# Tying the cached-sequence work of a decoder step to the attention blocks beside which it is emitted

## The chip, the cores and the metric

The kernel runs on one core of a Trainium2 chip. The metric is the device time of one execution in microseconds; the number for a kernel is the median of its runs. TensorE multiplies matrices, VectorE (DVE), ScalarE (ACT) and GpSimd (POOL) do the elementwise work, and most transfers are issued by SyncE (SP).

## The reference

One step of a small decoder: a recurrent layer (RG-LRU) and an attention layer (FoX) with a decay between positions. It is done for one new sequence of 2048 tokens (the prompt) and for 8 running sequences of 8 new tokens each, which have 4096 earlier tokens in a paged cache. 16 heads of 64. Cut to what matters here:

```python
def fox_block(q, k, v, cq, ck, q_pos, k_pos):
    s = jnp.einsum('bqhd,bkhd->bhqk', q, k).astype(jnp.float32) * (HEAD_DIM ** -0.5)
    s = s + jnp.swapaxes(cq, 1, 2)[:, :, :, None] - jnp.swapaxes(ck, 1, 2)[:, :, None, :]
    mask = k_pos[None, :] <= q_pos[:, None]
    s = jnp.where(mask[None, None], s, -jnp.inf)
    p = jax.nn.softmax(s, axis=-1)
    return jnp.einsum('bhqk,bkhd->bqhd', p.astype(v.dtype), v)

def run_group(x, rnn_state, conv_state, past_k, past_v, past_logf, pos0, ...):
    ...                     # recurrent layer, then shared keys and values of the new tokens
    k_all = jnp.concatenate([past_k.astype(k_new.dtype), k_new], axis=1)
    v_all = jnp.concatenate([past_v.astype(v_new.dtype), v_new], axis=1)
    ...
    y = fox_mixer(rms_norm(x, b_pre_norm[l]), k_all, v_all, cq, ck, q_pos, k_pos, b_w_in[l], b_w_out[l])
    x = x + rms_norm(y, b_post_norm[l])
```

`run_group` is called twice: for the prompt without a past, and for the running sequences with `cache_k[page_table]` and `cache_v[page_table]` as the past.

## The kernel before, in words

The kernel is written with a planner: the program emits instructions with tiles, and the planner then fixes the order of each engine's queue. It keeps a model of time; an engine takes the instruction emitted earliest among those whose data are ready in that model. Instructions emitted late can therefore be placed early. `together` emits a run of matmuls that stays together behind its first one. At run time each queue is in order.

The stages, in order: the recurrent layer of the first half of the tokens; the shared projections (`shared`, keys, values, queries, gate) of that half; the recurrent layer of the second half; its projections, in two parts of 512 tokens; the attention of the prompt (`attention`); the output projection (`project`).

The attention goes over 64 units, one for each head and each quarter `qc` of the queries. A unit has up to 16 score blocks of 128 keys by 512 queries: two matmuls into `st` (lines 1531 and 1532, and 1534 on the diagonal), the exponential on ScalarE into `p` (1540), and, for four blocks at a time and two blocks later, the products with the values into `ops` (1551) and the sums on GpSimd into `acc`. There are 640 score blocks. Ahead of a unit, `top` makes its row maxima: a matmul into `sx` (1404) and a reduction on VectorE, 1406 off the diagonal and 1408 on it. `top` runs up to 18 blocks ahead (`LEAD`). Score blocks rotate over two PSUM banks, `sx` over three, and `p` over 5 buffers (`NP`). Two more banks, tags `d` and `o`, belong to the decode and later to the projection.

The decode is the attention of the 8 running sequences to the cache. It has 16 turns, one for each sequence and half of the heads; two run beside the projections of the first half, 14 beside those of the second half and the attention. A turn loads 8 groups of 4 key pages and 8 of 4 value pages (`pages`, line 1072; a group is 1 MB, and keys and values share four `raw` buffers). Each key group is transposed by two instructions on VectorE (1157); after four groups, `scores` multiplies (1125 into `dS`). `softmax` follows, with a trip through DRAM (`pd`, `sx`), and then each value group is multiplied by `products` (1235 into `dO`), which waits for the four page transfers themselves. The turns overlap: `period` interleaves the keys of the next turn with the values of this one.

`Side` decides beside what the decode is emitted. `along` adds up the cost that the main work yields, and advances the decode until its own yielded cost is that sum times a share. The decode's cost units are `QK`, `PV` and `HOP`; a turn counts as `TURN` units:

```python
    QK, PV, HOP = 700.0, 255.0, 300.0
    TURN = 16 * QK + 33 * PV + 10 * HOP
```

The share is one number for the projections of the second half and for the attention; what isn't emitted by the end of the attention is emitted after it. After the decode, the same side work loads and splits the output projection's weights (`project_ready`).

Of the kernel before, what the change touches and what calls it, by code (L numbers as in the profile page):

```python
# [11 lines left out]
F32 = mybir.dt.float32  # L12
# [4 lines left out]
AX = mybir.AxisListType  # L17
# [3 lines left out]
P = 128  # L21
# [6 lines left out]
H = 16  # L28
# [15 lines left out]
B_ORDER += [("g", c) for c in range(4)]  # L44

SHARE = 1.13
LEAD = 18
RAMP = 8
NS = 3
# [2 lines left out]
AHEAD = 8  # L52
FIRST = 2
NACC = 5
NP = 5
ADD = "G"
OG = 1
NQ = 6
# [14 lines left out]


SYNC = mybir.DependencyInfo(mybir.DependencyClass.Sync, mybir.DependencyReason.DATA)


def f(ap):
# [5 lines left out]
def tile_hawk_fox(  # L84
# [8 lines left out]
    V, A, G, T, S = nc.vector, nc.scalar, nc.gpsimd, nc.tensor, nc.sync  # L93
# [9 lines left out]
    def tt(eng, out, a, b, op):  # L103
        eng.tensor_tensor(out, a, b, op=op)  # L104

    def together(mms, after=()):

        first = mms[0]().ins
        for d in after:
            tc.add_manual_dep(first, d.ins.name, SYNC)  # L110
        with tc.high_priority(), tc.issue_after(first):
            for mm in mms[1:]:
                mm()
# [97 lines left out]
    psum = {}  # L211
# [805 lines left out]
    TURN = 16 * QK + 33 * PV + 10 * HOP  # L1017
# [4 lines left out]
    def decode(es, turns, nraw, nktr, ahead):  # L1022
# [84 lines left out]
        def keys(t, xs):  # L1107

            dl = t.dl
            b, hg, gmx = t.b, t.hg, t.gmx  # L1110

            def fetch_c():
                sc = t.sc = pool.tile([P, NPG // 4, 8, 32], F32, name="sc", tag="sc")
                S.dma_start(sc[:, :, :, :].rearrange("p x h i -> p (x h i)"),
                            c_d[hg, :, :, b].rearrange("m a x f -> (m a) (x f)").unsqueeze(1).to_broadcast([16, DS, 8 * 256]))
                t.cn = pool.tile([DS, 8, DS], F32, name="cn", tag="cn")
                S.dma_start(t.cn[:, :, :], cn_d[hg * 8:(hg + 1) * 8, b * DS:(b + 1) * DS].unsqueeze(0).to_broadcast([DS, 8, DS]))

            def scores(g, pp, kt):

                sp = bank("dS", "d" if ahead or pp == 0 else "o")

                def score(h, x, a):
                    blk = (h * 2 + x) * 32
                    return T.matmul(sp[a * 32:(a + 1) * 32, h * P:(h + 1) * P], qw[:, pp * 2 + h // 2, h % 2 * 2 + x, :],  # L1125
                                    kt[:, :, a, blk:blk + 32], start=(x == 0), stop=(x == 1))

                together([partial(score, h, x, a) for h in range(4) for x in range(2) for a in range(4)])
                sv = t.sc[:, g * 4:(g + 1) * 4, pp * 4:(pp + 1) * 4, :].rearrange("p n h i -> p h n i")
                tt(V, sv, sp[:, :].rearrange("p (h n i) -> p h n i", h=4, n=4), sv, ALU.subtract)  # L1130
                V.tensor_reduce(gmx[:, g, pp * 4:(pp + 1) * 4], sv, axis=AX.XY, op=ALU.max)

            def new_scores(raw):
                kx = (spare() if ahead else pool.tile([P, 512], F32, name="kx", tag="kx"))[:, :512]
                V.transpose(kx, raw[:, :])
                sp = bank("dS")

                def score(h, x):
                    blk = (h * 2 + x) * 32
                    return T.matmul(sp[:32, h * DS:(h + 1) * DS], qw[:, h // 2, h % 2 * 2 + x, :], kx[:, blk:blk + DS],  # L1140
                                    start=(x == 0), stop=(x == 1))

                together([partial(score, h, x) for h in range(8) for x in range(2)])
                tt(V, t.cn[:, :, :], sp[:DS, :64].rearrange("p (h j) -> p h j", h=8), t.cn[:, :, :], ALU.subtract)
                tt(V, t.cn[:, :, :], t.cn[:, :, :], maskN[:, :].unsqueeze(1).to_broadcast([DS, 8, DS]), ALU.add)
                V.tensor_reduce(gmx[:DS, 2, :], t.cn[:, :, :], axis=AX.X, op=ALU.max)

            for x in xs:
                g, n = divmod(x, 4)
                if n == 0:  # L1150
                    t.kts = [pool.tile([P, 4, 4, 256], F32, name="ktr", tag="ktr", bufs=nktr) for _ in range(2)]
                raw, _ = pages(cache_k, b, hg, x)
                if x == (3 if ahead else 0):
                    fetch_c()
                    t.rown = new_rows(ks_d, b, hg)
                for pp in range(2):
                    V.transpose(t.kts[pp][:, n], raw[:, :, pp * 256:(pp + 1) * 256])  # L1157
                    if n == 3:
                        dl.after(1 + pp, lambda g=g, pp=pp, kt=t.kts[pp]: scores(g, pp, kt))
                    if (g, n, pp) == (1, 0, 0):  # L1160
                        new_scores(t.rown)
                    dl.tick()
                    yield QK
# [59 lines left out]
        def values(t, xs):  # L1223

            dl = t.dl
# [5 lines left out]
            def products(i, raw, came):  # L1231

                def mm(d, a):
                    c = ((i + d) % 2 * 2 + a) * 32
                    return T.matmul(op[c:c + 32, :256], sx[:, d, i // 4, a * 4:(a + 1) * 4, :].rearrange("p h q -> p (h q)"),  # L1235
                                    raw[:, d, a * 256:(a + 1) * 256],
                                    start=(i + d < 2), stop=(i + d == NPG - 1))

                together([partial(mm, d, a) for d in range(4) for a in range(2)], came)

            def new_products(raw):
                for a in range(2):
# [2 lines left out]

            for x in xs:
                raw, came = t.raws.pop(0) if t.raws else pages(cache_v, b, hg, x)
                dl.after(1, lambda i=x * 4, raw=raw, came=came: products(i, raw, came))
                if x == 5:
                    t.rown = new_rows(vs_d, b, hg)  # L1250
                yield 2 * PV
                dl.tick()
                yield 2 * PV
# [53 lines left out]
    def attention(es):  # L1307
# [86 lines left out]
        def top(u, j, ck):  # L1394
# [8 lines left out]
            ps = ps3.tile([P, 512], F32, name="sx", tag="sx", bufs=3)  # L1403
            T.matmul(ps[:, :w], qb[0:96, j * P:(j + 1) * P], kb[0:96, ck * 512:ck * 512 + w], start=True, stop=True)  # L1404
            if ck < qc:
                V.reduce_max(mx[:, j, ck:ck + 1], ps[:, :w], axis=AX.X)  # L1406
            else:
                V.tensor_tensor_reduce(ps[:, :w], ps[:, :w], maskb[:, 512 - w:], scale=1.0, scalar=NEG,
                                       op0=ALU.add, op1=ALU.max, accum_out=mx[:, j, ck:ck + 1])
# [110 lines left out]
            yield 300  # L1520
        ops = acc = None
        pair = []
        for u, (h, qc) in enumerate(units):
            load_low(u + 2)
            for k in range(nks[u]):
# [1 line left out]
                qa, qb = qas[u], qbs[u % NQ]  # L1527
                lo = max(0, k - qc * 4) * P
                ks = slice(k * P, (k + 1) * P)
                ps = ps3.tile([P, 512], F32, name="st", tag="st", bufs=2)  # L1530
                T.matmul(ps[:, lo:], ka[:, ks], qa[:, lo:], start=True, stop=False)  # L1531
                T.matmul(ps[:, lo:], kb[:, ks], qb[:, lo:], start=False, stop=(k < qc * 4))  # L1532
                if k >= qc * 4:
                    T.matmul(ps[:, lo:lo + P], identB[:, :], causal[:, :], start=False, stop=True)
# [41 lines left out]
    lent = {}  # L1576
# [207 lines left out]
    def beside():  # L1784
        yield from decode(dec, turns[FIRST:], 4, 2, True)
        dec.close()
        yield from project_ready(last)

    side = Side(beside())
# [3 lines left out]
    wkeep.close()  # L1793
    lin.close()
    psum["att"] = banks(att, "psa", 6)
    side.along(attention(att), share)
    side.upto(1e12)
    project(last)
    att.close()
# [36 lines left out]
```

## Time and profile before

| what | value |
|---|---|
| median of 3 runs | 3058.37 us (3051.74 to 3059.14) |
| the profiled execution | 3055.27 us, its span 3053.6 us |
| mean granted TensorE clock | 0.965 |
| bytes moved | 653.41 MB, mean 214 GB/s |
| second projections beside decode | about 1210 to 1692 us |
| attention, first to last score block | about 1725 to 2860 us |
| output projection, end | to 3053.6 us |

In the rows of the profile, a group has its line, engine, operation, output and inputs with shapes and count, then after the first bar its busy time and the mean of one in ns, and after the second bar the idle time of the engine just ahead of it and what ended that. The slice rows give tenths of busy time for 40 equal slices of 76.3 us. PE is TensorE's matmuls, PEld its weight loads. Matmul ends are modelled, so a busy PE isn't one at its peak.

### The profile page before, as it was taken

The page shows a single profiled execution, that of the slowest core. Times are in us where ns is not written, and L with a number is a line of the kernel's source. Part 1 is how long each engine was busy: PE and PEld are TensorE (multiplying, and loading weights), DVE is VectorE, ACT ScalarE, POOL GpSimd, SP SyncE. Part 2 cuts the span into 40 slices and gives each one's busy share as a digit, 9 for nine tenths or more (in the row PEclk, how much of TensorE's full clock was granted, in tenths as well). Part 3 has the DMA queues.
Part 4 walks back from the last instruction along what each step waited for, and adds up shares of the span by engine and source line. Part 5 has one row for each costly group of instructions (what it writes and reads, how often), then busy time and mean ns, then how long its engine had stood idle before and what let it go on. Part 6 is the DMA issues. An engine that isn't in the chain of part 4 may idle for free.

```text
span 3053.6 us, 60463 instructions
## 1 busy us (share of the span) xinstructions
PE 2827.0 (93%) x21614; PEld 2258.5 (74%) x21614; DVE 1810.2 (59%) x4012; ACT 1269.8 (42%) x2874; POOL 1079.6 (35%) x1199
## 2 busy tenths in 40 slices
PE   6998999999999989998999799899899899999898
PEld 5997789988999978896888456565556565565687
DVE  7876465425357766765555566676767675554344
ACT  4665442222346655433333144343444345455311
POOL 1653201000016532000000366556465557587522
PEclk9999999999999999999999799899999999999999
DMA  4224546788622256999999988999999998323243
GB/s 122 81 85 133 175 125 203 240 268 263 216 83 89 83 185 194 316 320 320 330 311 315 294 274 268 299 275 308 306 298 319 322 297 258 92 65 86 84 145 111
DMA packets 492864, 653.41 MB, mean 214 GB/s; under 512 B 91099, under 2 KB 292828, under 8 KB 485285
## 3 DMA queue, kind: packets, MB, share of 16 engines
q1 hardware_dynamic: 488934, 643.87, 67.1%
q10 hardware_dynamic: 3340, 3.56, 0.5%
q8 instruction: 171, 2.80, 0.4%
q0 software_dynamic: 288, 2.10, 0.2%
q14 instruction: 131, 1.07, 0.1%
HBM read 513.82 MB, written 135.16 MB: 213 GB/s over the span
## 4 chain that ended last, share of the span: by engine, by line
PE 59%; DMA 18%; DVE 9%; ACT 5%; SPq 4%; issue 3%; POOL 2%; DVEq 0%; ACTq 0%; POOLq 0%
PE ops L1551 6%; PE y L368 4%; PE y L366 4%; PE y L367 4%; DMA raw<-in_cache_v_dram 4%; PE kv L366 4%; PE kv L367 4%; PE kv L368 4%; DMA raw<-in_cache_k_dram 4%; PE st L1531 3%; PE sx L1404 3%; PE dO L1235 3%; PE dS L1125 2%; PE st L1532 2%; PE qg L366 2%
## 5 line engine op out<-in xcount | busy, mean ns | idle before, releaser
L104 POOL TENSOR_TENSOR acc<-acc,p 128x512 f32<-128x512 f32 (+3 forms) x576 | 638.7, 1109 | 419.2 <-PE ops L1551 271.1
L1540 ACT ACTIVATE p<-st 128x512 f32<-128x512 f32 (+3 forms) x576 | 289.5, 524 | 404.9 <-PE st L1532 198.8
L1157 DVE STREAM_TRANSPOSE ktr<-raw 128x1024 f32<-128x1024 f32 x256 | 305.7, 1225 | 160.2 <-DMA raw<-in_cache_k_dram 157.8
L1406 DVE TENSOR_REDUCE mxs<-sx 128x1 f32<-128x512 f32 x384 | 253.1, 679 | 119.7 <-PE sx L1404 118.3
L367 PE MATMUL kv<-wl,xh 128*128 128x256 f32 (+3 forms) x1088 | 309.3, 287 | 11.2 <-DVE wl L411 11.0
L366 PE MATMUL kv<-wh,xh 128*128 128x256 f32 (+3 forms) x1088 | 310.8, 290 | 5.9 <-ACT wh L410 5.4
L368 PE MATMUL kv<-wh,xl 128*128 128x256 f32 (+3 forms) x1088 | 309.4, 287 | 0.0
L1531 PE MATMUL st<-qa,ka 128*128 128x512 f32 (+3 forms) x640 | 273.9, 428 | 12.2 <-ACT p L1540 11.0
L1551 PE MATMUL ops<-p,vvt 128*64 128x256 f32 (+1 forms) x2176 | 261.0, 366 | 3.4 <-ACT p L1540 2.8
L1404 PE MATMUL sx<-kbt,qbt 96*128 96x512 f32 (+3 forms) x640 | 236.9, 425 | 26.1 <-DMA qbt<-qd 12.0
L1532 PE MATMUL st<-qbt,kbt 128*128 128x512 f32 (+3 forms) x640 | 239.3, 374 | 0.0
L410 ACT ACTIVATE wh<-wst,gv 128x256 fp32r<-128x256 f32 (+1 forms) x384 | 164.5, 499 | 179.9 <-DMA wst<-in_b_w_in_dram 62.1
L411 DVE SCALAR_TENSOR_TENSOR wl<-wst,gv,wh 128x256 fp32r<-128x256 f32 (+1 forms) x384 | 170.5, 493 | 105.5 <-ACT wh L410 104.0
L1551 PEld LDWEIGHTS ops<-p,vvt 128*64 128x64 f32 x2176 | 161.2, 140 | 92.6 <-issue 22.7
L366 PE MATMUL qg<-xh,wh 128*128 128x384 f32 (+2 forms) x640 | 228.9, 359 | 0.0
L368 PE MATMUL qg<-xh,wl 128*128 128x384 f32 (+2 forms) x640 | 227.4, 356 | 0.0
L367 PE MATMUL qg<-xl,wh 128*128 128x512 f32 (+2 forms) x640 | 226.9, 356 | 0.0
L367 PEld LDWEIGHTS kv<-wl,xh 128*128 128x128 f32 (+1 forms) x1088 | 204.3, 189 | 14.9 <-DVE wl L411 12.6
L366 PEld LDWEIGHTS kv<-wh,xh 128*128 128x128 f32 (+1 forms) x1088 | 204.2, 189 | 12.0 <-ACT wh L410 6.4
L1090 POOL TENSOR_TENSOR qw<-qb,amask 128x128 f32<-128x128 f32 x64 | 29.3, 464 | 509.9 <-PE dS L1125 266.4
L368 PEld LDWEIGHTS kv<-wh,xl 128*128 128x128 f32 (+1 forms) x1088 | 205.6, 189 | 4.1 <-issue 4.1
L1531 PEld LDWEIGHTS st<-qa,ka 128*128 128x128 f32 x640 | 124.0, 194 | 109.9 <-issue 53.0
(297 smaller groups left out, 6370.0 us busy)
## 6 DMA issues: line engine op xcount, KB each, us to landing
raw<-in_cache_k_dram SPq DMA_DIRECT2D x512, 256.0 KB
raw<-in_cache_v_dram SPq DMA_DIRECT2D x512, 256.0 KB
wst<-in_w_kv_dram SPq DMA_DIRECT2D x48, 512.0 KB
wst<-in_b_w_in_dram SPq DMA_DIRECT2D x48, 512.0 KB
xt<-in_x_prompt_dram SPq DMA_DIRECT2D x32, 512.0 KB
wst<-in_a_w_in_dram SPq DMA_DIRECT2D x64, 256.0 KB
out_dram<-kf SPq DMA_DIRECT2D x128, 128.0 KB
sc<-cd SPq DMA_DIRECT2D x16, 1024.0 KB
```

The source lines that it names most:

```text
L104: eng.tensor_tensor(out, a, b, op=op)
L366: T.matmul(ps, lh(k), rh(k), start=(k == 0), stop=False)
L367: T.matmul(ps, lh(k), rl(k), start=False, stop=False)
L368: T.matmul(ps, ll(k), rh(k), start=False, stop=(k == nk - 1))
L411: V.scalar_tensor_tensor(wl[:, k, :], st[:, k, :], gk, f(wh[:, k, :]), op0=ALU.mult, op1=ALU.subtract)
L1157: V.transpose(t.kts[pp][:, n], raw[:, :, pp * 256:(pp + 1) * 256])
L1404: T.matmul(ps[:, :w], qb[0:96, j * P:(j + 1) * P], kb[0:96, ck * 512:ck * 512 + w], start=True, stop=True)
L1406: V.reduce_max(mx[:, j, ck:ck + 1], ps[:, :w], axis=AX.X)
L1531: T.matmul(ps[:, lo:], ka[:, ks], qa[:, lo:], start=True, stop=False)
L1532: T.matmul(ps[:, lo:], kb[:, ks], qb[:, lo:], start=False, stop=(k < qc * 4))
L1540: pair.append((k, lo, p, A.activation(p[:, lo:], ps[:, lo:], AF.Exp)))
L1551: return T.matmul(ops[r * HD:(r + 1) * HD, a0 * P:], vvs[h % 2][:, k, :], p[:, :].rearrange("p (a r c) -> p a r c", a=2, r=2)[:, a0:, r, : ...
```

## The change

The first matmul of each score block of the attention, and each reduction of line 1406, is remembered as the current place on its engine. A decode transpose gets an order edge to the place on VectorE, and the first matmul of a score run and of a product run one to the place on TensorE, so that the planner can't put them ahead of it. An order edge holds within one engine's queue and adds no semaphore. Page loads, the softmax and the runs for the new rows get no edge. Nothing is tied before the attention, and nothing after it.

The share in the attention is worked out anew: what is left of the 14 turns, over 0.9 of the attention's own cost. The `p` buffers go from 5 to 6. The product run of value group 0 of a turn is emitted one tick later in these turns. Once the decode has been emitted, score blocks use the decode's two banks in turn with their own two.

```diff
+SPAN = 0.9
-NP = 5
+NP = 6
+ORDER = mybir.DependencyInfo(mybir.DependencyClass.NoSync, mybir.DependencyReason.DATA)
...
+    place = {}
+
+    def behind(engine, ins):
+
+        if engine in place:
+            tc.add_manual_dep(ins, place[engine].name, ORDER)
+
+    def together(mms, after=(), beside=False):
         first = mms[0]().ins
         for d in after:
             tc.add_manual_dep(first, d.ins.name, SYNC)
+        if beside:
+            behind("T", first)
...
-                together([partial(score, h, x, a) for h in range(4) for x in range(2) for a in range(4)])
+                together([partial(score, h, x, a) for h in range(4) for x in range(2) for a in range(4)], beside=True)
...
-                    V.transpose(t.kts[pp][:, n], raw[:, :, pp * 256:(pp + 1) * 256])
+                    behind("V", V.transpose(t.kts[pp][:, n], raw[:, :, pp * 256:(pp + 1) * 256]).ins)
...
-                together([partial(mm, d, a) for d in range(4) for a in range(2)], came)
+                together([partial(mm, d, a) for d in range(4) for a in range(2)], came, True)
...
-                dl.after(1, lambda i=x * 4, raw=raw, came=came: products(i, raw, came))
+                dl.after(2 if ahead and x == 0 else 1, lambda i=x * 4, raw=raw, came=came: products(i, raw, came))
...
-                V.reduce_max(mx[:, j, ck:ck + 1], ps[:, :w], axis=AX.X)
+                place["V"] = V.reduce_max(mx[:, j, ck:ck + 1], ps[:, :w], axis=AX.X).ins
...
+        wide = [0]
+
+        def scores_bank():
+
+            if dec_done:
+                wide[0] += 1
+                if wide[0] % 2:
+                    return psum["dec"].tile([P, 512], F32, name="st", tag="do"[wide[0] // 2 % 2], bufs=1)
+            return ps3.tile([P, 512], F32, name="st", tag="st", bufs=2)
...
-                ps = ps3.tile([P, 512], F32, name="st", tag="st", bufs=2)
-                T.matmul(ps[:, lo:], ka[:, ks], qa[:, lo:], start=True, stop=False)
+                ps = scores_bank()
+                place["T"] = T.matmul(ps[:, lo:], ka[:, ks], qa[:, lo:], start=True, stop=False).ins
...
     def beside():
         yield from decode(dec, turns[FIRST:], 4, 2, True)
         dec.close()
+        dec_done.append(True)
         yield from project_ready(last)
...
-    side.along(attention(att), share)
+    cost = sum(4.1 * 0.42 * (512 - max(0, k - qc * 4) * P) + 213 for qc in range(4) for k in range(4 * qc + 4)) * H
+    side.along(attention(att), ((16 - FIRST) * TURN - side.spent) / (cost * SPAN))
+    place.clear()
     side.upto(1e12)
```

More of the change, by code (lines that the diff above doesn't have):

```diff
@@ L104, in tt @@
         eng.tensor_tensor(out, a, b, op=op)
-    def together(mms, after=()):
+    place = {}
[3 more added lines that the diff above has]
+    def together(mms, after=(), beside=False):
         first = mms[0]().ins
@@ L1574, in attention @@
                 yield 4.1 * (512 - lo) * 0.42 + (done[0] - before) * 213
-    lent = {}
+    lent, dec_done = {}, []
     rows = [(NSAMP, None, x1s_d[:, :], ys_flat)]
```

## The prediction

> **What bounds the kernel now.** I read the page first (busy shares, slices, chain), then the stretches of the attention, then the groups of instructions and the waits inside them, and last the timeline around single waits. From the page:
>
> ```profile
> PE 2827.0 (93%) x21614; PEld 2258.5 (74%) x21614; DVE 1810.2 (59%) x4012; ACT 1269.8 (42%) x2874; POOL 1079.6 (35%) x1199
> PE   6998999999999989998999799899899899999898
> PEclk9999999999999999999999799899999999999999
> DMA  4224546788622256999999988999999998323243
> PE 59%; DMA 18%; DVE 9%; ACT 5%; SPq 4%; issue 3%; POOL 2%; DVEq 0%; ACTq 0%; POOLq 0%
> ```
>
> TensorE is busy nearly everywhere, but the dips of PE and PEclk lie in slices 19 to 33, where the DMA row is at 9. Then DMA falls to 3 while PE stays at 9. That is the boundary I need: cached-sequence work ("decode") runs beside the attention only up to about 2570 us, and the attention is alone after that. The stretches (columns: stretch, its length, busy time and count of PE, PEld, DVE, ACT, POOL, then clock, DMA share, GB/s), then score blocks (line 1531 alone) and page transposes (line 1157 alone):
>
> ```profile
> 1692.00:1750.00 58.00, 40.41 (x376) 26.58 (x376) 32.91 (x73) 11.11 (x30) 19.28 (x27) 0.71 1.05 310
> 1750.00:2500.00 750.00, 688.21 (x6748) 437.29 (x6748) 510.21 (x1038) 313.25 (x799) 417.00 (x406) 0.95 0.95 297
> 2650.00:2850.00 200.00, 190.14 (x1094) 115.72 (x1092) 85.44 (x205) 105.59 (x234) 159.53 (x145) 0.99 0.30 79
> ```
>
> ```profile
> 1750.00:2500.00 750.00, 166.33 (x386) 75.24 (x387) 0.95 0.95 297
> 2650.00:2850.00 200.00, 63.46 (x149) 28.20 (x149) 0.99 0.30 79
> 1725.00:2500.00 775.00, 173.09 (x401) 78.68 (x402) 0.95 0.95 298
> ```
>
> ```profile
> 1260.00:1692.00 432.00, 82.11 (x69) 0.96 0.98 323
> 1692.00:2500.00 808.00, 180.69 (x151) 0.93 0.96 298
> ```
>
> Alone, a score block with all that belongs to it costs 200 / 149 = 1.342 us. Beside the decode, 386 blocks at that price would be 518 us of the 750. The decode's own TensorE work there is the sum of the groups that write dO, dS, dres, dsum and dm:
>
> ```profile
> L1404 PE MATMUL sx<-kbt,qbt 96*128 96x512 f32 (+3 forms) x386 | 144.4, 423 | 11.0 <-DVE mxs L1406 7.2 <-ACT qbt L1423 2.4 <-DVE mxs L1408 0.3
> L1235 PE MATMUL dO<-raw,sx 128*32 128x256 f32 x1152 | 80.3, 398 | 25.3 <-DMA raw<-in_cache_v_dram 18.2 <-DMA raw<-in_cache_k_dram 3.3 <-DMA sx<-pd 2.2
> L1125 PE MATMUL dS<-ktr,qw 128*32 128x128 f32 x2240 | 69.5, 277 | 4.4 <-DVE ktr L1157 4.4
> L1140 PE MATMUL dS<-sy,qw 128*32 128x8 f32 x288 | 11.3, 179 | 4.3 <-DVE sc L104 4.3
> L1263 PE MATMUL dres<-sel,ob 128*128 128x16 f32 x72 | 9.5, 265 | 0.0
> L1243 PE MATMUL dO<-rawn,dpc 128*32 128x256 f32 x36 | 7.6, 427 | 0.0
> L1203 PE MATMUL dsum<-ddg,ones 128*128 128x64 f32 x18 | 3.5, 277 | 1.5 <-DVE ddg L104 1.5
> L1181 PE MATMUL dm<-ident,dmr 128*128 128x8 f32 x18 | 2.9, 235 | 1.0 <-DVE dmr L1180 1.0
> L1177 PE MATMUL dm<-ident,dmx 128*128 128x128 f32 x9 | 2.5, 276 | 2.1 <-DVE dmx L1175 2.1
> ```
>
> 80.3 + 69.5 + 11.3 + 9.5 + 7.6 + 3.5 + 2.9 + 2.5 = 187 us for 1152 / 128 = 9 turns, 20.8 us a turn. What is left, **750 - 518 - 187 = 45 us, is the excess of running the two together**, and it is all that this change can win in that stretch. It has two parts. Idle: 750 - 688.2 = 61.8, of which attention alone would have had 386 x (200 - 190.1) / 149 = 25.5, so 36 are extra; the rows above name them (25.3 ahead of the value products, nearly all on pages that had not landed, 4.4 + 4.3 ahead of the scores). The other 9 are matmuls at a lower clock. How a wait turns into clock shows in the timeline (start, length, engine and line):
>
> ```profile
> 1886.77 0.40 PE L1532 MATMUL st<-qbt,kbt 128*128 128x512 f32 x1
> 1888.97 1.07 PE L1235 MATMUL dO<-raw,sx 128*32 128x256 f32 x16 [1.80 <-DMA raw<-in_cache_v_dram]
> 1890.92 0.63 PE L1532 MATMUL st<-qbt,kbt 128*128 128x512 f32 x1
> 1895.90 0.39 PE L1532 MATMUL st<-qbt,kbt 128*128 128x512 f32 x1
> ```
>
> The same matmul takes 0.40 us before a 1.80 us wait for a value page, 0.63 after it, and 0.39 again 7 us later. [...]
>
> **The change, part by part.** *Placement.* Before, nothing ties a decode instruction to the attention; the planner takes it as soon as its data are there. By the program's own cost units the first phase (shared projections, 311,800 units) at the old share, 1.13 x 316,610 / 1,281,600 = 0.279, emits 87,000 units of decode; counted through the turn's order, that is 70 transposes, and 69 had run by 1692. So nothing crosses from the attention into that phase, and its time stays (0). In the attention (616,000 units) the old share emits 172,000 units, 107,000 of them by 2500 us, where 401 of 640 blocks are done: under 5 turns. Yet all 151 recorded transposes, 9.4 turns and more, had run. The decode runs twice as fast as it is emitted, which is why DMA is full. Afterwards each transpose, score group and product group has a lower bound, the block beside which it is emitted, so emission sets the pace.
>
> *The pace.* The new share is (316,610 - 87,000) / (616,000 x 0.9) = 0.414. A turn in fact yields 22,000 units, not 22,615 (the softmax yields 8 hops, not 10), so decode ends at 0.9 x (308,200 - 87,000) / 229,600 = 87% of the attention, and its last transposes, some 14,000 units earlier, at 81%, block 518. 154 transposes over 518 blocks instead of 151 over 401: 0.297 a block, not 0.377. A block then takes 1.342 + 0.297 / 16 x 20.8 = 1.73 us, so transposes come at 0.172 per us instead of 151 / 775 = 0.195: 12% slower. Of the 297 GB/s, attention's own part is 386 / 750 x (79 x 200 / 149) = 55; decode's 242 become 213, attention's 61: 275 GB/s, a share of 0.95 x 275 / 297 = 0.88. Not idle, but off the ceiling: the boundary stretch held 1.05 at 310 GB/s.
>
> *What returns of the 45.* Bounds: none (0.88 with bursts still queues), and all. I take six tenths, 27 us: the waits on pages (25.3 + 4.4, two thirds of the 45) should mostly go, with their clock, while the waits of the softmax chain (4.3 + 1.5 + 1.0 + 2.1, DVE, no DMA) stay.
>
> *The waits it adds.* Order edges on one engine add no semaphore. Behind a transpose wait all later reductions on DVE, and the sx banks they free; behind a product group, all attention matmuls. Both engines stand as they did before in that respect; cover is the pages ahead. 0.172 transposes per us are 0.086 key groups and as many value groups, one group of four pages per 5.8 us; with four raw buffers a group has about 17 us from its slot's release to its use. It needs about 8 (1883.25 to 1891.70):
>
> ```profile
> 1883.25 3.47 SPq L1072 DMA_DIRECT2D raw<-in_cache_k_dram  x4
> 1891.70 2.37 DVE L1157 STREAM_TRANSPOSE ktr<-raw 128x1024 f32<-128x1024 f32 x2 [5.84 <-DMA raw<-in_cache_k_dram]
> SPq L1392 <- PE st L1534: 31.0, 5, 12.1
> ```
>
> The last row (who SP's queue waited for, 1720 to 2500) is the threat: page loads are not pinned, but share SP's queue with the query loads, which hold it up to 12.1 us; five times, so I cost it at nothing and keep up to 5 x 3 us in the range.
>
> *The start.* Of 1692 to 1750, 17.6 us are idle at a clock of 0.71, most of it here:
>
> ```profile
> 1708.24 2.39 PE L1404 MATMUL sx<-kbt,qbt 96*128 96x128 f32 x6 [11.51 <-DMA qbt<-qd]
> ```
>
> With transposes held, no fresh pages are fetched beyond four buffers while qbt lands, at a DMA share of 1.05. Between 0 and -17; I take -5, nearest to the buffers being full already.
>
> *The small edits.* A sixth p buffer: ScalarE waits for POOL's adds below, and TensorE for ScalarE; 0 to -8, taken -3. Four score banks once decode is emitted, for the last 13% of the blocks: 0.13 x 640 x 1.342 = 112 us. Alone, 9.9 of 200 us are idle, 3.6 of them ahead of a score block on ScalarE (2650 to 2850):
>
> ```profile
> L1531 PE MATMUL st<-qa,ka 128*128 128x512 f32 (+3 forms) x149 | 63.5, 426 | 4.1 <-ACT p L1540 3.6
> 2570.00:2650.00 80.00, 18.06 (x43) 8.03 (x42) 0.96 0.42 116
> ```
>
> So 0 to -5, taken -2. Value group 0 delayed by one tick: its first product waits less for sx (2.2 above), -1. The end: the two banks are no longer free for the projection's first row, which before runs among the blocks, in the second row above: 80 - 43 x 1.342 = 22 us there are the split of the projection's weights and that row. Following the attention, its matmuls move and are not added, but its dependent chain may show: 0 to half of that, +11, taken +3.
>
> Sum: -27 - 5 - 3 - 2 - 1 + 3 = **-35 us**. Against the profiled execution's 3055.27 (span 3053.6) that is 3020; the median of the runs, 3058.37, stands 3 higher within a spread of 3051.74 to 3059.14, so I add 2 and forecast a median of **3022 us**. About 0.3% (9 us) is what a measurement of this kernel can tell from no change.
>
> **The rivals.** *All of the excess returns.* For it: after 2570 no wait is long and the clock is 0.99. Against it: 0.88 of DMA. -45 - 10 - 5 - 4 = -64, 2991. [...]
>
> *Nothing measurable returns.* Spreading the decode over more blocks only spreads the same waits: then the softmax and DVE waits, not pages, carry the excess. The row of 25.3 speaks against it. 3050 to 3065.
>
> *Slower: groups that wait in their place.* Today's planner puts a score group where it believes its transposes done. Pinned, it stands 700 / 0.414 = 1690 units, 1.8 blocks, 3.0 us of block time behind its last transpose on DVE, which is itself in line behind a reduction. If DVE runs more than 3 us behind TensorE there, TensorE stops, and reductions stop with it. Rows (waits, 1700 to 2570: total, times, longest):
>
> ```profile
> DVE ktr L1157 <- DMA raw<-in_cache_k_dram: 75.8, 37, 5.8
> ACT p L1540 <- POOL acc L104: 19.3, 16, 2.8
> PEld dS L1125 <- DVE ktr L1157: 5.5, 4, 3.2
> ```
>
> Four of 35 groups (2240 / 64) waited, 1.4 us each. If half of the 39 groups do, and as many product groups at the same price, 2 x 19 x 1.4 = 53 with nothing regained but half the page waits, -15, and the start's -5: +33, 3088. For it: DVE's 75.8 us on pages do happen in line. [...] Against it: pages have 17 us where 8 suffice.
>
> *A late end.* Decode's last 70 us (2500 to 2570) and the projection's weights fit from block 518 to about 593 of 640; it would cost only past 63 us of lag. Chance included in the slower case.
>
> **Chances.** Forecast 0.50 (own range 3005 to 3040), all returns 0.22, nothing 0.10, slower 0.18. Faster by over 0.3% is the first two: 0.72, with 0.10 same and 0.18 slower. The range takes in the full return with the start's bound (2978) and, since leaving out the whole slower case would leave nearly 2 in 10 on one side, its nearer part, up to 3070.
>
> **What would show it.** Right: transposes spread evenly until block 500 or later (about 2600 us), DMA at 8 rather than 9 in slices 23 to 33, the idle ahead of dO well under 25 us for the whole attention, clock 0.97 or more beside decode, blocks alone unchanged at 1.34 us. Wrong: idle ahead of dS or ahead of sx on DVE growing (slower rival); dO's waits unchanged at DMA 0.88 (nothing returns); transposes still finished by 2500 us (the pins do not bind); a gap ahead of the first projection matmul (late end).

## The result, and the profile after

The changed kernel takes **3050.7 us** (median of 20 runs, 3038.0 to 3057.28) against 3062.73 us for the kernel before in the same session (20 runs). The ratio is 0.9959, 95% interval 0.9946 to 0.9971: faster by 0.41%, some 12 us. The forecast was 3022 and 35 us. The profiled execution took 3044.43 us, its span 3042.6 us.

From the page of the changed kernel (busy times; slices of 76.1 us; the chain by engine):

```profile
PE 2818.0 (93%) x21614; PEld 2260.3 (74%) x21614; DVE 1801.1 (59%) x4012; ACT 1271.1 (42%) x2874; POOL 1080.0 (35%) x1199
PE   5998999999999989998999799899999999999998
PEclk9999999999999999999999799999999999999999
DMA  4224546788622265999999978898889898974343
PE 51%; DMA 15%; DVE 6%; ACT 4%; SPq 4%; issue 3%; POOL 1%; ACTq 0%; DVEq 0%; POOLq 0%
```

The DMA row is at 7 to 9 up to slice 35 (counted from 0), where before it fell to 3 after slice 33. The stretches of the changed kernel (length, busy time of PE, PEld, DVE, ACT, POOL, then clock, DMA share, GB/s), and score blocks alone (line 1552):

```profile
1260.00:1692.00 432.00, 403.56 (x3799) 348.70 (x3797) 254.17 (x492) 151.06 (x391) 14.86 (x30) 0.97 0.99 323
1692.00:1750.00 58.00, 40.69 (x284) 24.98 (x286) 30.13 (x70) 13.95 (x34) 18.94 (x25) 0.68 0.92 265
1750.00:2700.00 950.00, 880.00 (x8051) 563.46 (x8048) 613.35 (x1289) 418.02 (x1041) 564.70 (x544) 0.95 0.86 263
```

```profile
1700.00:2660.00 960.00, 223.73 (x520) 102.28 (x520) 0.93 0.86 264
1750.00:2700.00 950.00, 225.89 (x525) 102.95 (x526) 0.95 0.86 263
2725.00:2842.00 117.00, 35.64 (x88) 16.62 (x87) 0.97 0.39 107
```

Transposes in stretches of 200 us, first the last two of the kernel before (line 1157), then the changed one (line 1168):

```profile
2300.00:2500.00 200.00, 47.78 (x41) 0.96 1.01 323
2500.00:2700.00 200.00, 0.00 (x0) 0.98 0.56 164
```

```profile
1700.00:1900.00 200.00, 32.58 (x27) 0.88 0.83 247
2300.00:2500.00 200.00, 37.69 (x31) 0.95 0.88 267
2500.00:2700.00 200.00, 35.02 (x29) 0.97 0.87 264
```

The edges do what the change says. The last transpose ends at 2660 us, with 520 blocks done; 41 per 200 us became 31. The first projections are untouched (69 transposes by 1692 in both). DMA fell to 0.86 at 263 GB/s. Yet the time hardly moved. The groups of TensorE in 1750 to 2700 us say why:

```profile
L1552 PE MATMUL st<-qa,ka 128*128 128x512 f32 (+3 forms) x525 | 225.9, 431 | 11.6 <-ACT p L1561 10.9 <-ACT acc L1561 0.2
L1415 PE MATMUL sx<-kbt,qbt 96*128 96x512 f32 (+3 forms) x526 | 191.1, 416 | 19.9 <-DVE mxs L1419 12.4 <-DVE mxs L1417 4.2 <-DVE sgt L106 1.4
L1246 PE MATMUL dO<-raw,sx 128*32 128x256 f32 x1200 | 84.4, 401 | 17.5 <-DMA raw<-in_cache_v_dram 17.5
L1136 PE MATMUL dS<-ktr,qw 128*32 128x128 f32 x2432 | 78.3, 284 | 6.6 <-DVE cn L106 3.8 <-DVE ktr L1168 2.6
```

The value products still wait 17.5 us for pages (18.2 before). By the prediction's own working, 525 blocks at 1.342 us are 704.6; the decode's groups sum to 201.5 us for 9.38 turns (with the small ones: dres 10.7, dS for new rows 11.3, dO for new rows 7.1, dsum 4.0, dm 5.7); 950 - 704.6 - 201.5 = **44 us of excess, where before it was 45**. It did not return. The waits on pages (total, times, longest; then two of SP's queue, 1720 to 2700):

```profile
DVE ktr L1168 <- DMA raw<-in_cache_k_dram: 18.4, 9, 6.0
PE dO L1246 <- DMA raw<-in_cache_v_dram: 17.5, 9, 5.2
SPq L1083 <- DVE ktr L1168: 25.0, 15, 4.6
SPq L1083 <- PE dO L1246: 24.3, 10, 4.7
```

VectorE's waits on key pages fell from 75.8 us to 18.4, but they had reached TensorE only in part: it stood 11.0 us ahead of the matmuls into `sx` before, and 19.9 in the longer stretch now. TensorE's idle time beyond what the blocks alone have was 36 us before and is now 70.0 - 525 x 9.9 / 149 = 35. In place of VectorE's waits, page loads now stand in SP's queue for a buffer that a transpose has yet to release: 25.0 us in 15 times, against 5.7 in the kernel before (1720 to 2500):

```profile
SPq L1072 <- DVE ktr L1157: 5.7, 3, 3.2
```

From the issue of a group's first page to its use, the median went from 8.6 to 16.8 us for keys, but only from 10.0 to 11.6 for values. The key pages lie in the four `raw` buffers until the block to which their transposes are tied. That the value pages are issued late because of this is inferred, not seen in the single waits: of the nine late value groups, the loads of three stood in SP's queue for over 1 us for their buffer (those used at 1943.23, 2189.93 and 2342.18 us, 8.9 of the 17.5 us), all three for TensorE and none for a transpose. The loads of the other six came up late in that queue without such a wait of their own. (The softmax's `sy`, line 1067, takes one of the four buffers in turn as well.)

Split at the first score block, the last value product and the last score block: the score blocks from first to last took 1141.4 us before and 1117.1 after (-24.3). But 22.8 us of TensorE time among the blocks were the first matmuls of the output projection, which now follow: what is behind the last block grew from 186.7 to 202.5 (+15.8). The start gave -2.0, the work before it -0.5. Together -11.0, the difference of the spans.

### The profile page after: what moved, and what is told of

It is laid out like the page before. It is cut to its first block, busy times and chain, and to the rows that moved or that the text cites. A ratio compares the mean times of both kernels' runs of the same rounds, so it can differ in the third digit from the quotient of the medians.

```text
span 3042.6 us, 60436 instructions
## 1 busy us (share of the span) xinstructions
PE 2818.0 (93%) x21614; PEld 2260.3 (74%) x21614; DVE 1801.1 (59%) x4012; ACT 1271.1 (42%) x2874; POOL 1080.0 (35%) x1199
## 4 chain that ended last, share of the span: by engine, by line
PE 51%; DMA 15%; DVE 6%; ACT 4%; SPq 4%; issue 3%; POOL 1%; ACTq 0%; DVEq 0%; POOLq 0%
PE ops L1572 7%; PE st L1552 4%; PE sx L1415 4%; DMA raw<-in_cache_k_dram 3%; PE dO L1246 3%; PE y L379 3%; PE y L378 3%; PE y L377 3%; PE kv L378 3%; PE kv L377 3%; PE st L1553 3%; PE kv L379 3%; PE dS L1136 3%; DMA raw<-in_cache_v_dram 3%; SPq L1083 2%
## 5 line engine op out<-in xcount | busy, mean ns | idle before, releaser
L1572 PE MATMUL ops<-p,vvt 128*64 128x256 f32 (+1 forms) x2176 | 269.1, 374 | 3.8 <-ACT p L1561 3.6
```

Of the source, the lines that this page charges most:

```text
L1572: return T.matmul(ops[r * HD:(r + 1) * HD, a0 * P:], vvs[h % 2][:, k, :], p[:, :].rearrange("p (a r c) -> p a r c", a=2, r=2)[:, a0:, r, : ...
```

## The experiments

Every kernel was timed against the kernel before on the same chip; the ratio is to that. Lines are of the changed kernel.

**Pages left out.** Theory: the excess is waits on pages. The loads of the attention's pages are issued once and the buffer kept, in the changed kernel and in the one before:

```diff
+            if held:
+                return held[0][0], []
```

> The changed kernel, with the page loads of the attention left out: one raw tile, loaded once, serves every page of the decode from the start of the attention on (those pages' results are not the real ones). Everything else stands. Theory P (the excess beside the decode is waits for pages, and the change did not remove them because pages are now issued late): at least 25 of the some 50 us of excess go, so 3050 becomes 3025 or less, dO's idle ahead goes to 0, and the clock beside the decode rises from 0.95 to 0.98. Theory N (the excess comes from decode and attention taking turns on TensorE and DVE, pages matter little): 3038 to 3047, only dO's own 20 us of idle shrink and other waits take their place.

> The kernel before, with the page loads of the attention left out in the same way. Theory P: the 45 us of excess mostly go, 3062 becomes 3030 or less, since the planner's free order was held up by DMA alone. Theory N: 3045 to 3058.

`still_after`: 3013.46, ratio 0.9856 (0.9838 to 0.9874), 37 us better by median than the changed kernel. `still_before`: 3055.65, 0.9983 (0.9969 to 0.9998). With the edges, pages are worth 1.0%; without, 0.2%: there the planner, freed of loads, packs 9.9 turns of decode into 291 blocks (552 in the changed kernel), and other waits appear. So the prize was there, and the changed kernel without page waits reaches it, while its edges do not bring it by themselves. Which part of the change opens the way to it is not shown, since `still_after` has edges, share and small edits, and `still_before` none of them.

**The parts of the change.** `share_only` is the kernel before with the new share and no edge; `pins_share` is the changed kernel without the three small edits.

```diff
share_only (from the kernel before):
-    side.along(attention(att), share)
+    side.along(attention(att), ((16 - FIRST) * TURN - side.spent) / (cost * 0.9))
pins_share (from the changed kernel):
-NP = 6
+NP = 5
-                dl.after(2 if ahead and x == 0 else 1, ...
+                dl.after(1, ...
-            if dec_done:
+            if False:
```

> The kernel before with the new share alone, no order edges, five p buffers, two score banks. If the pace matters and not the placing (theory P or N alike say little here): the planner still takes decode early, so transposes end near 2500 us as before and the time is within 8 us of the kernel before. If emission had been what held the kernel back: as fast as the changed kernel, 3050.

> The changed kernel without its small edits: order edges and new share, but five p buffers, two score banks, no delayed value group. If the edges and the pace carry the gain: within 5 us of the changed kernel (3046 to 3056). If the gain is the small edits': 3058 to 3066, as before.

`share_only`: 3068.02, 1.0033 (1.0017 to 1.0050), slower; the planner still pulls the decode early (one transpose after 2500 us). `pins_share`: 3065.37, **1.0009 (0.9994 to 1.0025)**. The edges and the share together give nothing that can be measured; the 0.41% comes with the small edits. In `pins_share` the value products wait longer than before, in 1750 to 2700 us:

```profile
L1246 PE MATMUL dO<-raw,sx 128*32 128x256 f32 x1200 | 85.4, 405 | 35.8 <-DMA raw<-in_cache_v_dram 29.1 <-DMA raw<-in_cache_k_dram 3.4 <-DMA r<-rs 1.7
```

**The small edits, one undone at a time**, and the tie of the transposes undone.

```diff
narrow:        -            if dec_done:
               +            if False:
narrow_ylate:  as narrow, the projection's first matmuls tied behind the last score block
               +            behind("T", T.matmul(ps, lh(k), rh(k), start=(k == 0), stop=False).ins)
               -    place.clear()
np5:           -NP = 6
               +NP = 5
nodelay:       -dl.after(2 if ahead and x == 0 else 1, ...
               +dl.after(1, ...
pins_T:        -behind("V", V.transpose(...).ins)
               +V.transpose(...)
```

> The changed kernel without the two extra score banks; six p buffers, edges, share and the delay stay. Theory W (the gain is the extra banks of the last 88 blocks): 3060 to 3066, and those blocks take 140 us and more with the projection's first rows among them again. Theory B (the gain is the sixth p buffer, which helps all 640 blocks): 3049 to 3054.

> The same without the extra banks, and the projection's matmuls tied behind the last score block by an order edge, so that they stay out of the attention as they do with the extra banks. If the banks help by giving TensorE more room ahead of ScalarE: 3060 to 3066 as without them. If they help only because they keep the projection's first rows out of the last blocks: 3049 to 3054.

> The changed kernel with five p buffers. Theory B: 3058 or more. Theory W: 3048 to 3054.

> The changed kernel without the delay of value group 0. If the three small edits add up to the 15 us between the kernel with edges and share alone and the whole change, and banks and p buffer account for 6 and 7: 3050 to 3056, with the idle ahead of dO on sx back at some 3 us.

> The changed kernel with the edges on TensorE alone; transposes are free again. Theory S (value pages land late because key pages wait in the four raw buffers for their tied transposes, median 17 us from issue to use): buffers come free sooner, dO's idle ahead falls from 20 us to under 10, DVE's own waits for key pages rise again towards 70, and the time falls to 3035 to 3045. Rival (a transpose that waits in DVE's queue for its page costs as much as it wins): 3050 or more, with sx's waits for DVE larger.

| kernel | median us | ratio, 95% | what is undone, in us (changed kernel: 0.9959) |
|---|---|---|---|
| narrow | 3052.19 | 0.9979 (0.9965 to 0.9993) | banks, 6 |
| narrow_ylate | 3048.13 | 0.9965 (0.9948 to 0.9982) | banks, but projection late, 2 |
| np5 | 3054.07 | 0.9983 (0.9967 to 1.0000) | sixth p buffer, 7 |
| nodelay | 3051.58 | 0.9971 (0.9953 to 0.9990) | delay of group 0, 4 |
| pins_T | 3055.90 | 0.9987 (0.9972 to 1.0001) | ties of the transposes, 9 |

The last column is the difference of the ratios times 3060. No one of them stands clear of the changed kernel, except `pins_T` at the edge (its interval begins where that of the changed kernel ends). Their sum for the three small edits, 17, agrees with the step from `pins_share` to the whole, 0.0050 x 3060 = 15. `narrow_ylate` suggests that more than half of what the banks bring is that the projection no longer takes them among the blocks; that is not resolved.

With the transposes free (`pins_T`) the pace holds all the same (31 to 32 transposes per 200 us until 2500), since the score and product runs are tied; but the waits go back to VectorE (1750 to 2700):

```profile
DVE ktr L1168 <- DMA raw<-in_cache_k_dram: 110.9, 48, 6.3
PE mps L1432 <- DVE mrow L1428: 16.3, 10, 4.2
PE dO L1246 <- DMA raw<-in_cache_v_dram: 6.7, 5, 3.6
```

Value pages are in time now (6.7 us), and reductions stand behind key transposes instead, so that TensorE waits for row maxima (16.3). The waits moved as had been expected; the time, 3055.90, did not fall to the 3035 to 3045 that went with it.

**A fifth buffer.** Room for it was made by five `p` buffers, three `qa`, one `sgt`, and `cs` among the `p` buffers; `lean4` has only that, `lean5` the fifth `raw` buffer too.

```diff
-        yield from decode(dec, turns[FIRST:], 4, 2, True)
+        yield from decode(dec, turns[FIRST:], 5, 2, True)
```

> The control for the next run: the changed kernel with four raw buffers still, but leaner elsewhere to make room (five p buffers, three qa, one sgt, the sums' copy in a p buffer). Between the kernel with five p buffers and that before: 3053 to 3066.

> The same lean kernel with a fifth raw buffer. Theory L (page loads are held up by the number of buffers: a load is issued when a buffer comes free, and lands about 5 us later): dO's idle ahead and DVE's waits for key pages both fall by half or more, and the time is 10 to 20 us under the control. Theory D (the transfers themselves are too slow at that rate): within 5 us of the control.

Both 1.0308 (1.0287 to 1.0330 and 1.0288 to 1.0328). The fifth buffer did remove page waits at the same bytes, but the room cost 3%, and the control no longer resembles the kernel; `lean4` first, then `lean5` (1720 to 2800):

```profile
SPq L1402 <- PE st L1554: 80.2, 27, 11.5
DVE ktr L1168 <- DMA raw<-in_cache_k_dram: 37.1, 17, 4.9
PE dO L1246 <- DMA raw<-in_cache_v_dram: 16.3, 8, 4.3
PE mps L1431 <- DVE mrow L1427: 15.7, 6, 5.4
```

```profile
SPq L1402 <- PE st L1554: 102.2, 24, 17.2
DVE ktr L1168 <- DMA raw<-in_cache_k_dram: 17.7, 10, 4.8
PE dO L1246 <- DMA raw<-in_cache_v_dram: 3.4, 3, 1.4
PE mps L1431 <- DVE mrow L1427: 22.3, 9, 4.1
```

Query loads (line 1402) hold SP's queue for their buffers. What a fifth buffer is worth in the real kernel stays open.

**The span of the decode**, over 0.97 of the attention in place of 0.9.

```diff
-SPAN = 0.9
+SPAN = 0.97
```

> The changed kernel with the decode spread over 0.97 of the attention instead of 0.9: 7% fewer pages per us. Theory L and theory D alike: dO's idle ahead falls by some us. If nothing else is late at the end: 3040 to 3048. If the projection's weights and the decode's last chain now reach past the last score block: 3055 or more, with idle ahead of the projection's first matmul.

3044.83, 0.9966 (0.9941 to 0.9991): not to be told from 0.9. A still lower rate brings nothing either; the excess, 41 us for 9.5 turns, is much the same. The idle time ahead of dO on pages, which was expected to fall, grew from 17.5 to 26.0 us, and VectorE's waits on key pages from 18.4 to 37.1, at a share of 0.84 (1750 to 2740):

```profile
DVE ktr L1168 <- DMA raw<-in_cache_k_dram: 37.1, 13, 4.4
PE dO L1246 <- DMA raw<-in_cache_v_dram: 20.3, 10, 5.1
PE dO L1246 <- DMA raw<-in_cache_k_dram: 5.7, 1, 5.7
```

**Which pages, bytes or buffers.** Key loads alone or value loads alone left out; three `raw` buffers; and added copies.

```diff
k_still:  +            if still and cache is cache_k:
          +                return still[0][:, :].unsqueeze(1).to_broadcast([P, 4, 512]), []
v_still:  the same with cache_v, the products read a constant
raw3:     -        yield from decode(dec, turns[FIRST:], 4, 2, True)
          +        yield from decode(dec, turns[FIRST:], 3, 2, True)
extra:    +                if k % 4 == 0:
          +                    S.dma_start(ex_d[k // 4], kd_d[...][:, :, :192])
```

> The key page loads of the attention are left out (transposes, score products and value pages stay; the transposed numbers are a constant's), so the four raw buffers hold value pages alone. Theory 'buffers' (value pages land late because key pages keep the raw buffers until their tied transposes): idle ahead of dO on pages falls from 17.5 us to under 3, and nearly the whole 37 us of the run without any page loads come, 3015 to 3022. Theory 'traffic' (what is lost is lost to bytes in flight, whoever they belong to): half of the page bytes leave, so about half of the 37 comes, 3028 to 3036, and dO still waits 5 to 10 us.

> The value page loads of the attention are left out (the value products multiply a constant), so the four raw buffers hold key pages alone and dO waits for no page. 'Buffers': VectorE's waits on key pages fall from 18.4 us to under 3 too, and most of the 37 us comes, 3015 to 3025. 'Traffic': half, 3028 to 3036, with some of the key waits left.

> The changed kernel with three raw buffers in place of four; nothing else moves and the bytes are the same. 'Buffers': the lead of a page falls by a quarter, dO's and VectorE's page waits together grow from 36 us to over 80, and the kernel is 20 to 60 us slower than the changed one. 'Traffic': the loads come at the same mean rate and in shorter bursts; under 10 us slower.

> The changed kernel with 0.2 MB copied from DRAM to DRAM every four score blocks of the attention, into a scratch that nobody reads; the bytes of the decode stretch go up by about a tenth and the DMA share from 0.86 to about 0.95, the share of the kernel before. 'Traffic': the excess beside the decode grows by a good part of what the fall from 0.95 to 0.86 should have given, 10 to 27 us slower. 'Buffers': landing takes little longer, under 6 us slower.

`k_still`: 3019.39, 0.9855 (0.9823 to 0.9886). `v_still`: 3014.95, 0.9845 (0.9814 to 0.9875). Either half gives the whole of what leaving out both gives. What is left of the waits on pages is 2.7 us ahead of dO in `k_still` (under 3 was expected) and 4.2 us on VectorE in `v_still` (under 3 was expected too). That is nearly as the buffers' theory says; for the other, halving the bytes would have had to be as good as removing them. But both runs also halve what SP's queue has to issue (597 page loads in 1750 to 2700 us in the changed kernel, 324 and 280 in these), so they do not tell a shortage of buffers from a queue whose loads come late. `raw3`: 3079.16, 1.0057 (1.0038 to 1.0076), 30 us slower than the changed kernel with the same bytes. Its waits and stretch (1750 to 2700), and the stretch of `k_still`:

```profile
DVE ktr L1168 <- DMA raw<-in_cache_k_dram: 56.1, 22, 9.6
PE dO L1246 <- DMA raw<-in_cache_v_dram: 36.5, 20, 6.2
1750.00:2700.00 950.00, 855.38 (x7840) 543.37 (x7840) 594.50 (x1236) 398.28 (x987) 543.42 (x524) 0.94 0.84 254
```

```profile
1750.00:2700.00 950.00, 894.40 (x8325) 570.90 (x8325) 625.55 (x1331) 428.67 (x1069) 577.62 (x555) 0.97 0.64 190
```

In `raw3` the share is lower (0.84) and the waits are two and three times as long: it is not the share that makes them. `extra` (3088.15, 1.0079) did not do what it was for. Its copies read only keys that are ready early, so the planner issued all 160 between 427 and 985 us, ahead of the attention, and the attention began 31 us later; it says nothing on added bytes. Its attention, where nothing was added, shows an excess of 55 us, 11 more than the changed kernel: differences of that size between two builds' profiles mean little.

**A looser tie.** A transpose is tied to the fourth or the twelfth reduction before the newest.

```diff
-                place["V"] = V.reduce_max(...).ins
+                back_.append(V.reduce_max(...).ins)
+                if len(back_) > 12:
+                    place["V"] = back_[-1 - 12]
```

> A transpose is tied not to the newest reduction emitted but to the fourth before it, so a key page's buffer may come free somewhat earlier, while the pace still follows emission. Theory 'buffers': dO's waits on value pages fall from 17.5 us towards the 6.7 of the run with free transposes, VectorE's key waits rise by less than 20, and the kernel is 3 to 10 us faster than the changed one. Theory 'bytes at this rate': the waits only change places between VectorE and TensorE, within 4 us of the changed kernel.

> The same with the twelfth reduction before it. 'Buffers': value waits about as with free transposes, 5 to 10 us, key waits 40 to 90 us, time between lag4 and the kernel with free transposes (3056). 'Bytes at this rate': within 5 us of the changed kernel.

`lag4`: 3044.38, 0.9951 (0.9927 to 0.9974). Its waits did not go as expected: those on value pages stayed (20.5 us), and those on key pages rose to 53.1, by 35 where less than 20 was expected. `lag12`: **3039.72, 0.9940 (0.9922 to 0.9958)**, the fastest with all the work in it, and the fastest by median; its interval overlaps that of the changed kernel, so that it beats it is likely and not shown. It is clear of `pins_T`: a loose tie is better than none, where a time between `lag4` and `pins_T` was expected. Waits of `lag12` (1750 to 2700):

```profile
DVE ktr L1168 <- DMA raw<-in_cache_k_dram: 90.9, 35, 7.3
PE mps L1435 <- DVE mrow L1431: 21.6, 8, 7.4
PE sx L1416 <- DVE mxs L1418: 11.6, 18, 2.0
PE dO L1246 <- DMA raw<-in_cache_v_dram: 1.8, 1, 1.8
```

The value waits are gone (1.8 us), and 21.6 and 11.6 us stand ahead of row maxima and of matmuls into sx, which wait for reductions (4.3 and 4.2 in the changed kernel). This profile is of the slowest of its seven runs (3051.84), so its stretch says less than its median. With each transpose tied to the newest reduction or the fourth before it, the value waits in 1750 to 2700 us are 16.6 to 29.3 us in seven builds (changed, `pins_share`, `narrow`, `narrow_ylate`, `np5`, `nodelay`, `lag4`). They vanish only with the twelfth (1.8) or with no tie (6.7), and then VectorE waits for key pages instead. All profiles by the prediction's working (window of the decode, blocks, decode's matmuls, turns by their value products):

| kernel | window us | blocks | decode us | turns | us a turn | excess us |
|---|---|---|---|---|---|---|
| before | 750 | 386 | 187.1 | 9.0 | 20.8 | 45 |
| changed | 950 | 525 | 201.5 | 9.38 | 21.5 | 44 |
| pins_share | 950 | 520 | 201.9 | 9.38 | 21.5 | 50 |
| lag12 | 950 | 522 | 200.2 | 9.64 | 20.8 | 49 |
| pins_T | 950 | 520 | 192.5 | 9.5 | 20.3 | 60 |
| raw3 | 950 | 504 | 198.2 | 9.12 | 21.7 | 75 |
| k_still | 930 | 527 | 200.9 | 10.12 | 19.9 | 22 |
| v_still | 930 | 525 | 196.9 | 9.88 | 19.9 | 28 |
| still_after | 930 | 525 | 197.0 | 9.88 | 19.9 | 28 |

Pages cost the changed kernel 44 - 28 = 16 us of excess and, in the decode's own matmuls, which ran slower after a wait (16 value products took 1.94 us after 2.40 us and 1.07 after 1.50), (21.5 - 19.9) x 9.38 = 15. The other 28 are there without any page. Each figure rests on one profile and, by `extra`, may be some 10 us off.

## Why the prediction was wrong in size and right in sign

*The pace* held: last transposes at block 520 (forecast 518), decode's end at 552 (555), share 0.86 (0.88), 263 GB/s (275), blocks alone 117 / 88 = 1.33 us (1.34), the first projections unchanged.

*What returns of the 45* is the step that failed: forecast -27, measured about -1 in the profiles. In time, `pins_share`, which has the edges and the share alone, stands at +3 us (-2 to +8). The step's reason was that the waits on pages are made by DMA at a share of 0.95 and would go at 0.88; that was the author's estimate. They did not: the changed kernel still has them at 0.86, `span97` has longer ones at 0.84, and `raw3` has them two and three times as long at 0.84. At equal bytes the number of buffers matters (`raw3`, 30 us slower with three), and in these runs the edges decide only who waits: VectorE for key pages (75.8 us before, 110.9 in `pins_T`, 90.9 in `lag12`), or TensorE for value pages (17.5 us in the changed kernel). The prediction had that lead in hand, 17 us a group against 8 needed, and read it as a mean for both kinds. The mean was near, (74 x 16.8 + 86 x 11.6) / 160 = 14; but keys got most of it, and of 86 value groups a quarter had 9.3 us or less, against 17 supposed. "Behind a transpose wait all later reductions; cover is the pages ahead" named the cost (in the kernel before, two matmuls into `sx` were done by 1890.69 us while VectorE stood 5.84 us for a page, and the first of their reductions ran behind the two transposes, at 1893.99); that a page which waits for its place holds a buffer of the next one was missed. How the buffers make a page late stays open. Few late loads stood in SP's queue for over 1 us for their buffer: three of 18 groups in the changed kernel (8.9 of 35.9 us of waits), two of 48 in the kernel before (1.4 of 93.6 us). The rest came late in the order that the planner gave that queue, and no run changes this order alone. Whether bytes in flight play a part is open too, since `k_still` and `v_still` change buffers, queue and bytes together, and `extra` failed.

That pages make two thirds of what running the two together costs was a little high: they make 16 + 15 of 44 + 15, about half. The rest, with the softmax chain and the reductions, was rightly left. The clock beside the decode did not rise to 0.97 (0.95 as before), and the waits are still there. Where they are nearly gone it was 0.97 (`k_still`) and 0.96 (`v_still`).

*The start*: -5 forecast, -2 measured. Ahead of the first matmuls into sx TensorE still stands 11.4 us for transfers, 11.51 before, though the DMA share there fell from 1.05 to 0.92.

*The small edits* carry the whole gain, so that the sign came out right by parts that the forecast priced at -3 us together. As far as the main mechanism goes, that is luck. No run has them without the edges, so their worth is what they give beside them: sixth buffer -7, delay -4, banks with the moved projection -6, where -3, -1, and -2 + 3 were forecast. The last had the wrong sign: the projection's row costs 15.8 us behind the attention and 22.8 among its blocks, so it gains where +3 was to be paid. The parts are each within the uncertainty of one run; their sum, 15, is measured.

*The rivals.* "Nothing measurable returns" (0.10) is what edges and share do; its reason, that softmax and not pages carry the excess, holds for about half (28 us stay in `still_after`). "All returns" (0.22) did not come; even `k_still` and `v_still`, with pages in time, keep 22 and 28 us of the excess. "Groups that wait in their place" (0.18) did not come for the scores (idle ahead of dS 8.7 before, 6.6 after), but its sign is in the value products of `pins_share`, 35.8 us in 950 for 25.3 in 750, and in the changed kernel's sx, 19.9 for 11.0. *A late end* did not occur.

## What to carry to other kernels

Before lowering the rate of a stream to remove its waits, count what holds its buffers and what stands in the queue that issues its loads: an order that delays the consumer also delays the release (key pages took 16.8 us from issue to use here, 8.6 before), and can delay the next load of whoever shares the buffers. A wait that vanishes from one engine's row (76 to 18 us here) is worth nothing until the same resource is looked up in the rows of the others. And work that is emitted late is not thereby done late: the planner pulled the decode of `share_only` and the copies of `extra` ahead; in these runs only an edge held it.

## What the runs showed of the hardware

The clock fell after short waits, as the changed kernel's value products show. The 16 products of a group, with the wait ahead in brackets:

```profile
1943.23 1.93 PE L1246 MATMUL dO<-raw,sx 128*32 128x256 f32 x16 [5.17 <-DMA raw<-in_cache_v_dram]
2189.93 1.84 PE L1246 MATMUL dO<-raw,sx 128*32 128x256 f32 x16 [2.54 <-DMA raw<-in_cache_v_dram]
2231.98 1.94 PE L1246 MATMUL dO<-raw,sx 128*32 128x256 f32 x16 [2.40 <-DMA raw<-in_cache_v_dram]
2633.05 1.24 PE L1246 MATMUL dO<-raw,sx 128*32 128x256 f32 x16 [2.20 <-DMA raw<-in_cache_v_dram]
2324.33 1.07 PE L1246 MATMUL dO<-raw,sx 128*32 128x256 f32 x16 [1.50 <-DMA raw<-in_cache_v_dram]
```

After 2.40 us or more the group took 1.84 to 1.94 us, after 1.50 us 1.07; 2.20 lies between, with 1.24, and in the kernel before a wait of 1.80 left the group at 1.07 and slowed what followed it (a matmul of 0.40 us took 0.63). It is tempting to read a length of wait from this at which the clock falls. The granted clock says otherwise. In these two traces it stood at 1.00 or 0.50, and its changes lie whole steps of 3.41 us apart. Around two of these groups (length of the step, busy time of PE, PEld, DVE, ACT, POOL, then clock, DMA share, GB/s):

```profile
2227.64:2231.05 3.41, 1.94 (x36) 1.49 (x35) 3.10 (x7) 1.82 (x5) 0.01 (x1) 1.00 1.13 340
2231.05:2234.46 3.41, 2.48 (x18) 1.20 (x19) 0.00 (x0) 0.00 (x0) 0.00 (x0) 0.50 0.92 174
2630.42:2633.83 3.41, 1.21 (x18) 0.42 (x17) 1.29 (x2) 0.19 (x1) 1.72 (x2) 1.00 0.93 276
2633.83:2637.25 3.42, 3.42 (x19) 2.21 (x13) 0.92 (x3) 0.87 (x2) 0.46 (x1) 0.50 1.07 389
```

Much of the wait of 2.40 us lay in the step before 2231.05, where the clock fell, and its products ran at 0.50. The wait of 2.20 us lay in the step before 2633.83; its products began at 1.00, at 2633.05, and ended at 0.50. Between 1695 and 2850 us the clock fell 20 times, each time after a step in which TensorE was idle for 1.16 to 2.99 us in all. No other step at full clock had more than 1.30 us. In seven of the 20 no single idle stretch inside the step was over 0.95 us, while elsewhere stretches of up to 1.23 us brought no fall. In the kernel before, 14 falls follow 0.95 to 2.81 us, and steps with up to 1.63 us are followed by none. So these records, whose matmul ends are modelled, show no sharp limit, neither for a single wait nor for the sum of a step.
